# A mixture-of-experts layer on one core: expert weights in loads of 2 MB with 16 KB per partition, eleven slot pairs, and norm 2 vectors and second expert bias on SyncE's queue

## The chip, the cores and the metric

The kernel runs on one core of a Trainium2 chip. The metric is the device time of one execution in microseconds. The kernel before takes 1097.09 us (median of three runs, 1096.65 to 1097.22). TensorE is PE, VectorE DVE, ScalarE ACT, GpSimd POOL, and SyncE SP; SP does nothing but issue transfers.

## The reference, cut to what matters

One encoder layer on 256 tokens of 1,024 features, all in float32: gated linear attention, a residual layer norm, a mixture of 32 experts of which each token takes four, and a second residual layer norm.

```python
h = _gla_mixer(x, w_in, gate_w2, gate_b, norm_g, w_out)        # 4 heads, key 128, value 256
x = _layer_norm(ALPHA * x + h, ln1_g, ln1_b)
logits = x @ router_w + router_b
top_v, top_i = lax.top_k(logits, 4); gates = softmax(top_v)
for e in range(32):
    y = _clamped_swiglu(x @ w_gu[e] + b_gu[e]) @ w_down[e] + b_down[e]   # w_gu[e] 1024x2048, w_down[e] 1024x1024
    out = out + combine[:, e:e+1] * y
x = _layer_norm(ALPHA * x + out, ln2_g, ln2_b)
```

All 32 experts have tokens, so all weights of `w_gu` (268 MB) and `w_down` (134 MB) pass from HBM to SBUF once: 402.65 MB.

## The kernel before

**Stages.** The attention comes first (to about 130 us), then the first norm, the router and the gather of the tokens of expert 0 (to about 155 us), then a loop over the 32 experts, and the second norm with its stores. In the loop the at most 64 tokens of an expert are gathered by 48 small matmuls with `xp` (the tokens in three bfloat16 parts) as the stationary operand (`gather`, L750), go through `first_product` (L769: 64 matmuls, `pgu`, into two PSUM banks), `swiglu` (L787, with four transposes `paT`), and `second_product` (L803: 32 matmuls, `py`), and are scattered into four banks `acc` that stay open over all experts. The gather of expert e+1 and the scatter of expert e-1 stand between the two products. `last_expert` (L817) has finer steps, and the second norm follows it.

**Weights.** A "chunk" is 1 MiB, 128 partitions of 8 KB. Expert e has 12: eight of `w_gu` (128 rows of 2,048 values, one row of 8 KB to a partition, contiguous) and four of `w_down` (256 rows, two rows of 4 KB to a partition). `weight` (L78) issues one DMA per chunk on SP's queue. In the last expert the four `w_down` chunks hold half rows, in runs of 2 KB, and the last of them comes as two DMAs.

**Slots.** 23 slots of 1 MiB (`slot`, L38, tags s0 to s22) hold everything big: the attention's inputs, weights and results first, and then the weight chunks. `order` (L74) is the order in which the slots are taken for weights. `load_next` (L109) issues the next chunk into the next slot of the ring; the issue waits on SP until the slot's last reader is done. 11 chunks of expert 0 are issued from places inside the attention, and four loads of the output projection `wo` (`load_wo`, L405) stand among them, in slots 21, 2, 15 and 12. The rest of the first 23 is issued at L876. From there each consumed chunk is followed by one `load_next`. SP works strictly in order, and a DMA also waits until the eighth DMA before it on the queue has landed (eight semaphores in turn).

**Other vectors.** Norm 2's scale and shift are read on ACT's queue as two rows, after the load of chunk 324; four matmuls and four copies (L975 to L981, end of expert 29) spread them over 128 partitions; `rows` and `ln2` take two slots of the ring for this. The second expert bias `bdn` is loaded on ACT's queue in expert 0 (L734) and used by eight matmuls in expert 1 (L957).

**Overflow.** After expert 30 a branch (L885) looks whether an expert has more than 64 tokens; with these inputs it is not taken.

The order of the work is the order of the code: nothing is rescheduled.

Of the kernel before, what the change touches and what calls it, by code (L numbers as in the profile page):

```python
# [20 lines left out]
NSLOT = 23  # L21
NCH = 12
# [3 lines left out]
def encoder_kernel(ctx, tc, x, ln1_g, ln1_b, ln2_g, ln2_b, w_in, gate_w2, gate_b, norm_g, w_out,  # L26
# [4 lines left out]
    ring = ctx.enter_context(tc.tile_pool(name="ring", bufs=1))  # L31
# [6 lines left out]
    def slot(i, name, shape=(P, 2048), dt=F32):  # L38
        return ring.tile(list(shape), dt, name=name, tag=f"s{i}")
# [34 lines left out]
    order = [3, 18, 20, 6, 11, 7, 9, 4, 19, 13, 14, 21, 22, 2, 15, 5, 12, 17, 8, 16, 10, 1, 0]  # L74
# [3 lines left out]
    def weight(s, name, e, c, last=False):  # L78
        if last and c >= 8:
            t = slot(s, name, (P, 4, 512))  # L80
            h, j = divmod(c - 8, 2)
            n = 1 + (c == 11)
            for i in range(n):
                m = 4 // n
                sync.dma_start(t[:, i * m:(i + 1) * m, :],
                               dram(w_down, e * D * D + (j * 4 + i * m) * P * D + h * 512,
                                    [[D, P], [P * D, m], [1, 512]]))
            return t
        if c < 8:
            t = slot(s, name, (P, 2 * D))  # L90
            src = dram(w_gu, 0, [[2 * D, P], [1, 2 * D]])
            o = c * P * 2 * D
            big = D * 2 * D
        else:
            t = slot(s, name, (P, 2, D))
            src = dram(w_down, 0, [[D, P], [P * D, 2], [1, D]])
            o = (c - 8) * 2 * P * D
            big = D * D
        src = bass.AP(tensor=src.tensor, offset=src.offset + o + e * big, ap=[list(a) for a in src.ap])
        sync.dma_start(t, src)  # L100
        return t

    def next_slot():
        order.append(order.pop(0))
        return order[-1]

    late = {}

    def load_next():  # L109
        i = nload[0]  # L110
        if i == NCH * (NE - 5) and "ln2" not in late:
            if "rows" in late:
                late["ln2"] = slot(order.pop(0), "ln2", (P, 2, D))
                return
            late["rows"] = rows = slot(order.pop(0), "rows", (2, D))
            act.dma_start(rows[0:1], dram(ln2_g, 0, [[D, 1], [1, D]]))
            act.dma_start(rows[1:2], dram(ln2_b, 0, [[D, 1], [1, D]]))
        elif i < NCH * NE:
            chunks[i] = weight(next_slot(), f"w{i}", i // NCH, i % NCH, i // NCH == NE - 1)
            nload[0] += 1  # L120

# [13 lines left out]
    lnr = mis[:16, 1712:1840]  # L135
# [30 lines left out]
    sync.dma_start(rw, dram(router_w, 0, [[NE, P], [P * NE, 8], [1, NE]]))  # L166
    sync.dma_start(rbb, dram(router_b, 0, [[0, P], [1, NE]]))
    sync.dma_start(lnr[0:8], dram(ln1_g, 0, [[P, 8], [1, P]]))
    sync.dma_start(lnr[8:16], dram(ln1_b, 0, [[P, 8], [1, P]]))
# [43 lines left out]
    n = 0  # L213
# [47 lines left out]
    for c in range(4):  # L261
        hi, lo = wqk[c]
        for h in range(H):
            for j in range(2):
                cs = slice(j * 512 + h * DK, j * 512 + (h + 1) * DK)
                for kk in range(2):
                    k = 2 * c + kk
                    mm3(pqk[h][:, j * L:(j + 1) * L], hi[:, kk, cs], lo[:, kk, cs], xT[0][:, k, :], xT[1][:, k, :],
                        j == 0 and k == 0, k == 7)
        if c == 1:  # L270
            pt = bank(0, "plnT")
            pe.transpose(pt[:, :16], lnr, ident[:16, :16])
            dve.tensor_copy(lnT, pt[:, :16])
# [39 lines left out]

    for _ in range(4):
        load_next()
# [102 lines left out]

    vv = []
    score_level(-1)  # L420
    score_store(-1)
    for lev in range(7):
        score_level(lev)
        advance(lev)
        if lev == 0:
            load_next()
        proj(2 * lev)
        step(dve)
        if lev == 1:
            act.dma_start(bp, bass.AP(tensor=bd.tensor, offset=bd.offset, ap=[[2 * D, 96], [1, 2 * D]]))  # L430
        proj(2 * lev + 1)
        if lev < 6:
            step(dve)
        if lev == 1:
            vv.append(slot(8, "vv", (P, 2, D)))
        elif lev == 4:
            load_wo(21)
        elif lev == 5:
            load_wo(2)
        elif lev < 6:  # L440
            load_next()
            if lev == 2:
                load_next()
    step_wo(5, pool)
    load_wo(15)
# [6 lines left out]
    load_next()  # L452
    load_next()
    preload(AF.Sigmoid)
    proj(14)
    load_wo(12)
# [293 lines left out]
    def gather(pcol, xg):  # L750
# [18 lines left out]
    def first_product(chunk, xg, pgl, bias, after=None, between=None, split=False):  # L769
# [3 lines left out]
        for k in range(8):  # L773
            w = chunk(k)
# [6 lines left out]
            if after:  # L781
                after()
# [4 lines left out]
    def swiglu(pgl, aT, post=()):  # L787
# [6 lines left out]
        for c in range(4):  # L794
            if c % 2 == 0:
                cs = slice(c * P, (c + 2) * P)
                dve.tensor_mul(s[:, cs], l[:, cs], s[:, cs])  # L797
            pe.transpose(pb[:, c * P:(c + 1) * P], s[:, c * P:(c + 1) * P], ident)  # L798
# [4 lines left out]
    def second_product(chunk, y, aT, after=None):  # L803
        py = misc("py")
        for c in range(4):
            w = chunk(8 + c)
            for j in range(2):
                kk = 2 * c + j
                a0 = (kk % 4) * P + (kk // 4) * CAP
                for h in range(2):  # L810
                    mm(py[h * 64:(h + 1) * 64, :], aT[:, a0:a0 + CAP], w[:, j, h * 512:(h + 1) * 512],
                       kk == 0, kk == 7)
            if after:
                after()
        act.activation(y, py, AF.Copy)  # L815

    def last_expert(pgl, chunk, after):  # L817
# [16 lines left out]
        def quarter(h, c, i):  # L834
            w = chunk(8 + 2 * h + c)
# [40 lines left out]
    while nload[0] < NSLOT:  # L876
        load_next()

# [3 lines left out]
    def overflow():  # L882
        hold = order[:4]
        many = nc.values_load(cnt[0:1, 0:1], min_val=0, max_val=L)
        with tc.If(many > CAP):  # L885
# [4 lines left out]
            with tc.For_i(0, NE, 1) as e:  # L890
                pg = work.tile([P, 2, 2], F32, name="pg", bufs=1)
                row = slot(hold[2], "row", (1, 2 * D))
# [8 lines left out]
                for r in range(1, L // CAP):  # L901
                    dve.tensor_scalar(pg[:, 0, :], pg[:, 0, :], float(CAP), None, op0=OP.subtract)
                    p_, g_ = (lambda t: pg[:, 0, t:t + 1]), (lambda t: pg[:, 1, t:t + 1])
                    own = slot(hold[3], "own")
# [5 lines left out]
                    def chunk(c):  # L910
                        return weight(hold[c % 2], f"o{r}_{c}", e, c)
# [12 lines left out]
    for e in range(NE):  # L924
# [23 lines left out]
        if e == 0:  # L948
            open_tiles()
            pt = misc("pgT")  # L950
# [24 lines left out]
        if e == NE - 3:  # L975
            rows, ln2 = late["rows"], late["ln2"]
            for j in range(2):
# [10 lines left out]
    z = slot(next_slot(), "z", (P, 2, D))  # L988
# [64 lines left out]
```

## Time and profile before

| | us |
|---|---|
| median of three runs | 1097.09 |
| the profiled execution, own time | 1101.22 |
| its span | 1099.4 |
| PE / DVE / ACT busy in the span | 1007.1 / 292.4 / 156.8 |
| DMA queue 1 (all of SP's and most transfers), share of 16 engines | 94.9% |
| w_gu loads, issue to landing (median of 256) | 19.9 |
| PE waiting for a w_gu load, in total | 61.5 |

A share of DMA is the time that packets took, over 16 engines; it can pass 1 because packets overlap a little. A packet is one contiguous run of one partition's data. "idle before <-X" names what ended an engine's idle time. Times of single executions differ by some microseconds from the median, as the profiled one does here.

### The profile page before, as it was taken

What the parts mean: (1) busy time and instruction counts of PE and PEld (TensorE: products, weight loads), DVE (VectorE), ACT (ScalarE), POOL (GpSimd) and SP (SyncE); (2) the same over time, 40 slices, a digit from 0 to 9 for tenths busy, and PEclk for the clock granted to TensorE, in tenths of its full rate; (3) what the DMA queues carried; (4) which work ended last, traced back from release to release, by engine and by line L of the source; (5) the groups of instructions that cost most, each with busy time, mean ns of one, the idle gap of its engine ahead of it and who ended that gap; (6) DMA issues with size and microseconds to landing.
All of it is one profiled execution on the core that took longest, in us unless ns stands there. A gap on an engine that the chain in (4) does not pass through costs nothing. (4 is left out here: it accounts for less than half of the span.)

```text
span 1099.4 us, 14219 instructions
## 1 busy us (share of the span) xinstructions
PE 1007.1 (92%) x6002; PEld 432.5 (39%) x6002; DVE 292.4 (27%) x639; ACT 156.8 (14%) x272; POOL 43.2 (4%) x45
## 2 busy tenths in 40 slices
PE   7999979999999999989899988888899998888995
PEld 6988743433333333323333333322233333333331
DVE  4786574112111122101111111110111111111104
ACT  5545431000000000000000000000000000000102
POOL 4202320000000000000000000000000000000001
PEclk8999989999999999999999999999999999999998
DMA  9956689999999999999999999999999999999992
GB/s 340 351 200 215 265 317 368 418 417 417 416 416 417 417 415 417 416 418 418 417 417 417 417 416 416 417 417 417 417 418 418 417 417 417 416 416 417 416 398 99
DMA packets 82954, 425.24 MB, mean 387 GB/s; under 512 B 8979, under 2 KB 9763, under 8 KB 50118
## 3 DMA queue, kind: packets, MB, share of 16 engines
q1 hardware_dynamic: 81936, 422.23, 94.9%
q10 hardware_dynamic: 950, 2.04, 0.6%
q8 instruction: 49, 0.80, 0.3%
q14 instruction: 19, 0.16, 0.0%
HBM read 422.81 MB, written 1.44 MB: 386 GB/s over the span
## 5 line engine op out<-in xcount | busy, mean ns | idle before, releaser
L51 PE MATMUL pgu<-w,sx 128*64 128x512 f32 (+1 forms) x2056 | 476.1, 601 | 62.0 <-DMA w<-in_moe_w_gu_dram 61.5
L51 PEld LDWEIGHTS pgu<-w,sx 128*64 128x64 f32 x2056 | 140.9, 137 | 378.2 <-issue 227.4
L51 PE MATMUL py<-w,ya 128*64 128x512 f32 x1024 | 227.2, 595 | 1.4 <-ACT ya L799 0.9
L789 DVE TENSOR_SCALAR gl<-pgu 128x512 f32<-128x512 f32 x31 | 21.4, 691 | 675.2 <-PE pgu L51 675.2
L51 PEld LDWEIGHTS py<-w,ya 128*64 128x64 f32 x1024 | 70.9, 137 | 151.9 <-issue 124.6
L51 PE MATMUL pxg<-oh,xp 128*128 128x64 bf16 x1536 | 51.4, 194 | 1.6 <-DVE oh L616 0.7
L51 PEld LDWEIGHTS <-xp 128*128 128x128 bf16 x1536 | 50.4, 99 | 4.3 <-issue 3.2
L815 ACT ACTIVATE ya<-py 128x512 f32<-128x512 f32 x31 | 18.5, 597 | 231.8 <-PE py L51 231.8
L767 ACT ACTIVATE wgf<-pW 128x256 f32<-128x256 f32 x16 | 6.1, 384 | 270.4 <-PE pW L766 270.4
L767 ACT ACTIVATE wT<-pW 128x256 f32<-128x256 f32 x16 | 6.1, 382 | 253.2 <-PE pW L766 253.2
L51 PE MATMUL pvo<-step,xTh 128*128 128x512 f32 x128 | 40.2, 395 | 0.0
L1016 POOL TENSOR_TENSOR z<-z,ln 128x512 f32<-128x512 f32 x1 | 1.3, 1265 | 938.8 <-ACT z L1014 938.8
L51 PE MATMUL acc<-ya,wT 64*128 64x512 f32 x128 | 36.1, 641 | 0.0
L51 PE MATMUL acc<-ya,wgf 64*128 64x512 f32 (+1 forms) x124 | 36.1, 641 | 0.0
L799 ACT ACTIVATE ya<-paT 128x512 f32<-128x512 f32 x31 | 18.5, 597 | 67.3 <-PE paT L798 67.3
L748 DVE TENSOR_TENSOR sx<-sx,lnT 128x256 f32<-128x256 f32 x64 | 27.2, 425 | 2.2
L747 DVE TENSOR_TENSOR sx<-pxg,lnT 128x256 f32<-128x256 f32 x64 | 26.7, 418 | 0.2 <-PE pxg L51 0.2
L797 DVE TENSOR_TENSOR sx<-gl,sx 128x256 f32<-128x256 f32 x62 | 23.7, 422 | 6.7 <-ACT sx L790 3.6
L51 PEld LDWEIGHTS pvo<-step,xTh 128*128 128x128 f32 x128 | 23.5, 188 | 4.4
L51 PE MATMUL pvo<-step,xTl 128*128 128x512 f32 x64 | 24.9, 389 | 0.0
L51 PE MATMUL ph<-wos,o2T 128*128 128x512 f32 x96 | 23.9, 398 | 0.7 <-ACT o2T L59 0.7
L791 DVE TENSOR_SCALAR gl<-pgu 128x512 f32<-128x512 f32 x31 | 21.4, 691 | 5.0 <-PE pgu L51 5.0
(235 smaller groups left out, 691.0 us busy)
## 6 DMA issues: line engine op xcount, KB each, us to landing
w<-in_moe_w_gu_dram SPq DMA_DIRECT2D x256, 1024.0 KB, 19.9
w<-in_moe_w_down_dram SPq DMA_DIRECT2D x127, 1024.0 KB, 20.0
wqk<-in_gla_w_in_dram SPq DMA_DIRECT2D x4, 1024.0 KB, 10.8
wv<-in_gla_w_in_dram SPq DMA_DIRECT2D x4, 1024.0 KB, 7.1
wog<-in_gla_w_in_dram SPq DMA_DIRECT2D x4, 1024.0 KB, 7.4
wo<-in_gla_w_out_dram SPq DMA_DIRECT2D x4, 1024.0 KB, 7.7
xs<-in_x_dram SPq DMA_DIRECT2D x4, 256.0 KB, 5.1
w<-in_moe_w_down_dram SPq DMA_DIRECT2D x2, 512.0 KB, 14.0
```

Source lines behind the costliest of these rows:

```text
L51: pe.matmul(o, l, r, start=start, stop=stop, skip_group_check=True)
L747: dve.tensor_mul(o, i, g)
L748: dve.tensor_add(o, o, b)
L767: return lambda: act.activation(wT, pb[:, :L], AF.Copy)
L789: dve.tensor_scalar(g, pgl[0], 7.0, None, op0=OP.min)
L791: dve.tensor_scalar(l, pgl[1], 7.0, -7.0, op0=OP.min, op1=OP.max)
L797: dve.tensor_mul(s[:, cs], l[:, cs], s[:, cs])
L799: act.activation(aT, pb, AF.Copy)
L815: act.activation(y, py, AF.Copy)
L1016: pool.tensor_mul(zh, zh, ln2[:, 0, halves[1]])
```

## The change

Expert weights now come in pairs of chunks: 2 MiB, 16 KB per partition, each partition's 16 KB contiguous in HBM. For `w_gu` partition p of pair c holds rows 256c+2p and 256c+2p+1; for `w_down` it holds four consecutive rows. An expert has six such loads (`NCH` 6), and there are eleven pair slots and one single slot. The contraction index of a matmul therefore steps through every second row (fourth row for `w_down`), so the other operand is read with that step: `column_block` picks every second column of `xs` and of `xp` for the transposes and the gathers, and `swiglu` transposes every fourth column of its result, after one DVE product over 512 columns instead of two over 256. The router weights and the first norm's vectors are laid out the same way. In the last expert the last `w_gu` pair comes as two DMAs of 8 KB runs, and each `w_down` pair as two or three DMAs of 2 KB runs, as before.

The 23 slots are declared in a pool of their own in the order (11, 7), (4, 9), (19, 21), (2, 15), (12, 13), (14, 22), (3, 18), (20, 6), (5, 17), (16, 8), (1, 10), 0. It is closed after the gather of expert 0, and the ring's eleven pairs r0 to r10 and the single slot lie at those addresses. All first loads of weights are issued there; none stands inside the attention any more. The four `wo` loads are issued before the attention's levels, into slots 3, 18, 20 and 6. Norm 2's vectors are loaded once behind the first eleven pairs, on SP's queue, spread over 128 partitions by the DMA (2 x 0.5 MB) into the single slot; the four matmuls and copies are gone. `bdn` is loaded on SP's queue.

```diff
-NSLOT = 23
-NCH = 12
+NPAIR = 11
+NCH = 6
...
+    for i in (11, 7, 4, 9, 19, 21, 2, 15, 12, 13, 14, 22, 3, 18, 20, 6, 5, 17, 16, 8, 1, 10, 0):
+        slot(i, f"home{i}")
...
+    def weight(t, e, c, last=False):
+        if last and c >= 4:
+            for i in range(2):
+                n = 1 + (c == 5 and i == 1)
+                for q in range(n):
+                    m = 4 // n
+                    sync.dma_start(t[:, i, q * m:(q + 1) * m, :],
+                                   dram(w_down, e * D * D + (i * 4 + q * m) * P * D + (c - 4) * 512,
+                                        [[D, P], [P * D, m], [1, 512]]))
             return t
+        src, o, big = (w_gu, c * 2 * P * 2 * D, D * 2 * D) if c < 4 else (w_down, (c - 4) * 4 * P * D, D * D)
+        if last and c == 3:
+            for i in range(2):
+                sync.dma_start(t[:, i, :], dram(src, o + e * big + i * 2 * D, [[4 * D, P], [1, 2 * D]]))
         else:
+            src = bass.AP(tensor=src.tensor, offset=src.offset + o + e * big, ap=[[4 * D, P], [1, 4 * D]])
+            sync.dma_start(t.rearrange("p j n -> p (j n)"), src)
...
+    def column_block(a, k):
+        return a.rearrange("p (c q j) -> p c j q", c=4, j=2)[:, k // 2, k % 2, :]
...
-    for _ in range(4):
-        load_next()
...
+    for i in (3, 18, 20, 6):
+        load_wo(i)
...
-                mm(pb[:, k * CAP:(k + 1) * CAP], xp[:, i // 3, i % 3, k * P:(k + 1) * P], oh[:, i // 3, :],
+                mm(pb[:, k * CAP:(k + 1) * CAP], column_block(xp[:, i // 3, i % 3, :], k), oh[:, i // 3, :],
                    i == 0, i == 5)
...
         for k in range(8):
-            w = chunk(k)
+            w = chunk(k // 2)[:, k % 2, :]
...
-            if after:
+            if after and k % 2:
                 after()
...
+        dve.tensor_mul(s, l, s)
+        for r in range(4):
+            pe.transpose(pb[:, r * P:(r + 1) * P], s.rearrange("p (q r) -> p r q", r=4)[:, r, :], ident)
...
-    while nload[0] < NSLOT:
+    early.close()
+    ring.append(ctx.enter_context(tc.tile_pool(name="ring", bufs=1, side="right", reuse_waits="tile")))
+    while nload[0] < NPAIR:
         load_next()
+    ln2 = ring[0].tile([P, 2, D], F32, name="ln2", tag="single")
+    for j, a in enumerate((ln2_g, ln2_b)):
+        sync.dma_start(ln2[:, j, :], dram(a, 0, [[0, P], [1, D]]))
...
             open_tiles()
+            sync.dma_start(tmp["bdn"], dram(b_down, 0, [[D, NE], [1, D]]))
...
-        if e == NE - 3:
-            rows, ln2 = late["rows"], late["ln2"]
-            for j in range(2):
-                for c in range(2):
-                    pb = misc("pln2")
-                    mm(pb, ident[0:2, j:j + 1].to_broadcast([2, P]), rows[:, c * 512:(c + 1) * 512], True, True)
-                    act.activation(ln2[:, j, c * 512:(c + 1) * 512], pb, AF.Copy)
```

**On SP's queue during the attention**, before: behind the last attention weights come nine expert chunks, with the `wo` loads among what follows. The names in brackets are what each issue waits for: DMAHW is an earlier landing, the others are readers of the slot.

```order
L100 DMA w_525<-in_moe_w_gu_dram 128x2048 [waits DMAHW3_49,PE_49,Pool_49]
L100 DMA w_527<-in_moe_w_gu_dram 128x2048 [waits DMAHW6_49]
L100 DMA w_529<-in_moe_w_gu_dram 128x2048 [waits DMAHW7_49,PE_49]
L100 DMA w_531<-in_moe_w_gu_dram 128x2048 [waits DMAHW2_49,DMAHW0_49,DVE_49]
L100 DMA w_567<-in_moe_w_gu_dram 128x2048 [waits DMAHW1_49,DVE_49]
L100 DMA w_603<-in_moe_w_gu_dram 128x2048 [waits DMAHW3_49,DVE_49]
L100 DMA w_705<-in_moe_w_gu_dram 128x2048 [waits DMAHW5_49,DMAHW4_49,DVE_49]
L100 DMA w_707<-in_moe_w_gu_dram 128x2048 [waits DMAHW5_49,PE_49]
L100 DMA w_762<-in_moe_w_down_dram 128x2x1024 [waits DMAHW6_49,DVE_49]
L408 DMA wo_817<-in_gla_w_out_dram 128x4x512 [waits DMAHW7_49,DVE_49]
```

The same place after the change:

```order
L414 DMA wo_552<-in_gla_w_out_dram 128x4x512 [waits DMAHW2_49,PE_49,Pool_49]
L414 DMA wo_554<-in_gla_w_out_dram 128x4x512 [waits DMAHW6_49]
L414 DMA wo_556<-in_gla_w_out_dram 128x4x512 [waits DMAHW7_49,PE_49]
L414 DMA wo_558<-in_gla_w_out_dram 128x4x512 [waits DMAHW0_49,DVE_49]
L110 DMA w_1359<-in_moe_w_gu_dram 128x4096 [waits DMAHW4_49,DMAHW3_49,DVE_49]
L110 DMA w_1361<-in_moe_w_gu_dram 128x4096 [waits DMAHW5_49,DVE_49]
L110 DMA w_1363<-in_moe_w_gu_dram 128x4096 [waits DMAHW6_49,DVE_49]
L110 DMA w_1365<-in_moe_w_gu_dram 128x4096 [waits DVE_49,DMAHW7_49,PE_49,Pool_49]
L110 DMA w_1367<-in_moe_w_down_dram 128x4096 [waits DMAHW0_49,DMAHW1_49,DVE_49,PE_49]
L110 DMA w_1369<-in_moe_w_down_dram 128x4096 [waits DMAHW1_49,PE_49]
```

The four `wo` loads take the place of the first four chunks, and every weight load is twice as large and waits for the readers of two slots.

**On SP's queue at the start of the expert loop**, after the change, the vectors of norm 2 stand behind the eleventh pair (w_1379) and `bdn` (L944) behind the fifteenth (w_1460). Before, neither was on this queue.

```order
L110 DMA w_1379<-in_moe_w_down_dram 128x4096 [waits DMAHW6_49,PE_49]
L871 DMA ln_1381<-in_ln_g_dram 128x1024 [waits DVE_49,DMAHW7_49,PE_49,Pool_49]
L871 DMA ln_1381<-in_ln_b_dram 128x1024 [waits DMAHW0_49]
L110 DMA w_1401<-in_moe_w_down_dram 128x4096 [waits DMAHW1_49,PE_49]
L110 DMA w_1421<-in_moe_w_gu_dram 128x4096 [waits DMAHW2_49,PE_49]
L110 DMA w_1448<-in_moe_w_gu_dram 128x4096 [waits DMAHW3_49,PE_49]
L110 DMA w_1460<-in_moe_w_gu_dram 128x4096 [waits DMAHW4_49,PE_49]
L944 DMA bdn<-in_moe_b_down_dram 32x1024 [waits DMAHW5_49,DVE_49]
```

Both are queued in order with the weights, so a wait of theirs holds the next pair back.

**On PE at the end of expert 29**, before: the second product takes four chunks, and the spread of the norm's rows (`pln`) stands ahead of expert 30's bias.

```order
L798 MATMUL paT<-ident,sx 128x128 x4
L51 MATMUL acc<-ya,wT 128x512 x2
L51 MATMUL py<-w_5900,ya 64x512 x4
L51 MATMUL py<-w_5913,ya 64x512 x4
L51 MATMUL py<-w_5919,ya 64x512 x4
L51 MATMUL py<-w_5925,ya 64x512 x4
L51 MATMUL pln_6223<-rows,ident 128x512
L51 MATMUL pln_6226<-rows,ident 128x512
L51 MATMUL pln_6229<-rows,ident 128x512
L51 MATMUL pln_6232<-rows,ident 128x512
L51 LDWEIGHTS sel
```

After the change:

```order
L788 MATMUL paT<-ident,sx 128x128 x4
L59 MATMUL acc<-ya,wT 128x512 x2
L59 MATMUL py<-w_5543,ya 64x512 x8
L59 MATMUL py<-w_5560,ya 64x512 x8
L59 LDWEIGHTS sel
```

The matmuls of the two products are as many as before, each load feeds twice as many, and `pln` is gone.

## Rows read from the trace of the kernel before

**Rows 1.** Stretches: PE, PEld, DVE, ACT, POOL busy (instructions), granted clock, DMA share, GB/s
```profile
0.00:60.00 60.00, 53.29 (x331) 48.38 (x332) 37.16 (x68) 31.01 (x42) 19.09 (x30) 0.94 0.93 344
60.00:153.00 93.00, 86.96 (x485) 73.38 (x483) 65.05 (x113) 47.37 (x81) 21.28 (x13) 0.98 0.66 247
153.00:190.00 37.00, 34.75 (x203) 13.47 (x202) 21.70 (x46) 6.42 (x13) 0.00 (x0) 0.91 0.85 321
190.00:1060.00 870.00, 804.98 (x4876) 288.21 (x4874) 155.90 (x390) 65.42 (x124) 0.00 (x0) 1.00 1.02 417
```

**Rows 2.** Who PE waited for, 400 to 1080 us: us in total, times, longest us
```profile
PE pgu L51 <- DMA w<-in_moe_w_gu_dram: 61.5, 111, 1.7
```

**Rows 3.** PE in order of time, expert 2: start us, us, operation, count
```profile
216.11 0.60 PE L51 MATMUL pgu<-bp,sel 96*64 96x512 bf16 x4
216.54 13.90 PE L51 MATMUL pgu<-w,sx 128*64 128x512 f32 x64
...
230.65 1.56 PE L51 MATMUL pxg<-oh,xp 128*128 128x64 bf16 x48
...
234.85 7.09 PE L51 MATMUL py<-w,ya 128*64 128x512 f32 x32
241.77 0.60 PE L51 MATMUL pgu<-bp,sel 96*64 96x512 bf16 x4
```

**Rows 4.** Stretches in which only 8 KB runs, or only 4 KB runs, flow
```profile
230.00:246.00 16.00, 16.00 (x120) 6.60 (x118) 3.99 (x9) 2.10 (x4) 0.00 (x0) 1.00 1.01 420
250.00:256.50 6.50, 6.24 (x32) 1.89 (x28) 0.19 (x1) 0.00 (x0) 0.00 (x0) 1.00 1.02 409
...
381.00:397.00 16.00, 16.00 (x117) 6.36 (x114) 5.20 (x13) 1.50 (x3) 0.00 (x0) 1.00 1.01 420
401.60:407.00 5.40, 5.40 (x28) 1.85 (x26) 0.00 (x0) 0.00 (x0) 0.00 (x0) 1.00 1.03 410
```

**Rows 5.** DMA packets of 230 to 246 us, and of 250 to 256.5 us
```profile
DMA packets 921, 6.72 MB, mean 420 GB/s; under 512 B 102, under 2 KB 102, under 8 KB 102
DMA packets 686, 2.66 MB, mean 409 GB/s; under 512 B 37, under 2 KB 37, under 8 KB 686
```

**Rows 6.** The page's DMA: all packets; the queue of instruction fetches (packets, MB, share)
```profile
DMA packets 82954, 425.24 MB, mean 387 GB/s; under 512 B 8979, under 2 KB 9763, under 8 KB 50118
...
q8 instruction: 49, 0.80, 0.3%
```

**Rows 7.** SP's queue: when loads were issued (start us, us to the last issue's end, count)
```profile
86.25 8.91 SPq L408 DMA_DIRECT2D wo<-in_gla_w_out_dram  x3
...
119.72 0.34 SPq L100 DMA_DIRECT2D w<-in_moe_w_gu_dram  x1
...
143.57 0.90 SPq L100 DMA_DIRECT2D w<-in_moe_w_down_dram  x2
153.24 6.45 SPq L100 DMA_DIRECT2D w<-in_moe_w_down_dram  x2
161.11 21.09 SPq L100 DMA_DIRECT2D w<-in_moe_w_gu_dram  x8
183.59 5.95 SPq L100 DMA_DIRECT2D w<-in_moe_w_down_dram  x4
```

**Rows 8.** POOL's last piece of wo, in order of time
```profile
130.61 2.39 POOL L60 TENSOR_TENSOR wos<-wo,wos 128x1024 fp32r<-128x1024 f32 x1 [2.99 <-ACT wos L59]
```

**Rows 9.** PE in order of time, expert 29 to the end of the last first product
```profile
1022.29 3.78 PE L51 MATMUL pln<-rows,ident 2*128 2x512 f32 x8
...
1056.27 0.62 PE L51 MATMUL pgu<-bp,sel 96*64 96x512 bf16 x4 [2.73 <-PEq L885]
...
1068.68 5.38 PE L51 MATMUL pgu<-w,sx 128*64 128x512 f32 x32
```

**Rows 10.** Attention scores, level 0 (every second column read) and whole columns: min/median/max ns
```profile
L51 PE MATMUL psc<-QT,KQ x16: 334/337/337, 48.3 to 50.8; 128*128 128x128 f32 x16
...
L51 PE MATMUL psc<-KQ x16: 273/275/275, 46.5 to 48.2; 128*128 128x128 f32 x16
```

More of the change, by code (lines that the diff above doesn't have):

```diff
@@ L1 @@
+from contextlib import ExitStack
 import concourse.bass as bass
@@ L29, in encoder_kernel @@
     dve, act, pe, pool, sync = nc.vector, nc.scalar, nc.tensor, nc.gpsimd, nc.sync
-    ring = ctx.enter_context(tc.tile_pool(name="ring", bufs=1))
+    early = ExitStack()
+    slots = early.enter_context(tc.tile_pool(name="slots", bufs=1, side="right"))
     fixed = ctx.enter_context(tc.tile_pool(name="fixed", bufs=1))
@@ L38, in slot @@
     def slot(i, name, shape=(P, 2048), dt=F32):
-        return ring.tile(list(shape), dt, name=name, tag=f"s{i}")
+        return slots.tile(list(shape), dt, name=name, tag=f"s{i}")
+    for i in (11, 7, 4, 9, 19, 21, 2, 15, 12, 13, 14, 22, 3, 18, 20, 6, 5, 17, 16, 8, 1, 10, 0):
+        slot(i, f"home{i}")
     def keep(shape, name, dt=F32, tag=None):
@@ L71, in copy @@
             dve.tensor_copy(o, a)
-    order = [3, 18, 20, 6, 11, 7, 9, 4, 19, 13, 14, 21, 22, 2, 15, 5, 12, 17, 8, 16, 10, 1, 0]
+    ring = []
+    order = list(range(NPAIR))
     chunks = {}
     nload = [0]
[L78 to L87, printed above, removed]
-            return t
[L89 to L93, printed above, removed]
-        else:
[L95 to L100, printed above, removed]
-        return t
@@ L103, in next_slot, with pair, hold_pair @@
[L103 to L107, printed above, removed]
+    def pair(name, shape):
+        order.append(order.pop(0))
+        return hold_pair(order[-1], name, shape)
+    def hold_pair(j, name, shape):
+        return ring[0].tile([P, *shape], F32, name=name, tag=f"r{j}")
+    def weight(t, e, c, last=False):
[7 more added lines that the diff above has]
+                                        [[D, P], [P * D, m], [1, 512]]))
+            return t
+        src, o, big = (w_gu, c * 2 * P * 2 * D, D * 2 * D) if c < 4 else (w_down, (c - 4) * 4 * P * D, D * D)
+        if last and c == 3:
+            for i in range(2):
+                sync.dma_start(t[:, i, :], dram(src, o + e * big + i * 2 * D, [[4 * D, P], [1, 2 * D]]))
+        else:
+            src = bass.AP(tensor=src.tensor, offset=src.offset + o + e * big, ap=[[4 * D, P], [1, 4 * D]])
+            sync.dma_start(t.rearrange("p j n -> p (j n)"), src)
+        return t
@@ L109, in load_next, with chunk_shape @@
+    def chunk_shape(c, last=False):
+        return (2, 2 * D) if c < 4 else (2, 4, 512) if last else (4, D)
     def load_next():
         i = nload[0]
[L111 to L119, printed above, removed]
+        if i < NCH * NE:
+            e, c = divmod(i, NCH)
+            last = e == NE - 1
+            chunks[i] = weight(pair(f"w{i}", chunk_shape(c, last)), e, c, last)
@@ L424, in encoder_kernel @@
         advance(lev)
-        if lev == 0:
-            load_next()
         proj(2 * lev)
@@ L804, in second_product @@
         py = misc("py")
-        for c in range(4):
-            w = chunk(8 + c)
-            for j in range(2):
-                kk = 2 * c + j
-                a0 = (kk % 4) * P + (kk // 4) * CAP
+        for c in range(2):
+            w = chunk(4 + c)
+            for r in range(4):
+                a0 = r * P + c * CAP
                 for h in range(2):
-                    mm(py[h * 64:(h + 1) * 64, :], aT[:, a0:a0 + CAP], w[:, j, h * 512:(h + 1) * 512],
-                       kk == 0, kk == 7)
+                    mm(py[h * 64:(h + 1) * 64, :], aT[:, a0:a0 + CAP], w[:, r, h * 512:(h + 1) * 512],
+                       c + r == 0, c + r == 4)
             if after:
@@ L882, in overflow @@
     def overflow():
-        hold = order[:4]
+        hold = order[:3]
         many = nc.values_load(cnt[0:1, 0:1], min_val=0, max_val=L)
@@ L891, in overflow @@
                 pg = work.tile([P, 2, 2], F32, name="pg", bufs=1)
-                row = slot(hold[2], "row", (1, 2 * D))
+                own = hold_pair(hold[2], "own", (4 * D,))
+                row = own[0:1, 2 * D:]
                 with nc.allow_non_contiguous_dma(reason="a column"):
@@ L987, in encoder_kernel @@
     nb2 = work.tile([P, 1], F32, name="nb2", bufs=1)
-    z = slot(next_slot(), "z", (P, 2, D))
+    z = pair("z", (2, D))
     halves = [slice(0, 512), slice(512, 1024)]
```

44 lines of the change are left out of this document (13 added, 31 removed).

## The prediction, made before the changed kernel ran

> **What bounds the kernel now.** I read the stretches first. From 190 to 1060 us the 16 DMA engines are full (share 1.02) at a steady 417 GB/s, while before that they are not: 0.93, 0.66 and 0.85 of three stretches [rows 1]. PE looks busy too, at 805 of 870 us, so the second view is whom PE waits for: in 111 pieces, 61.5 us in all, for `w_gu` loads [rows 2]. The third view is PE's own time for an expert whose weights are already there. In expert 2 it is 25.7 us from one bias matmul (216.11) to the next (241.77), without a wait [rows 3]. An expert is 12.58 MB, which takes the DMA 30.2 us at 417 GB/s. So PE is faster than the queue by some 4.5 us an expert, eats up the lead of the filled ring, and then waits. The loop is bound by the transfers, and the time is: when the queue becomes full for good, plus the bytes that are left over the rate, plus what follows the last `w_gu` chunk.
>
> The end has to be checked by itself. PE spends 3.8 us on the spread of the norm's rows at 1022, 2.7 us in the branch, and finishes the first product of expert 31 at 1074.1 [rows 9]. How far behind the last landing that is, no row says. With 4.5 us of slack an expert against 3.8 and 2.7 us lost, I take it that PE and the queue about meet there, so what the queue gains the end gains.
>
> **Part 1, longer runs.** The trace has pure stretches: between 230 and 246 us hardly a packet is under 8 KB, between 250 and 256.5 us all are [rows 5]. Six 8 KB stretches lie at 419 to 421 GB/s and six of 4 KB at 407 to 411; two of each are shown [rows 4]. With means of 420.2 and 409.3 a packet holds one of 16 engines for 8192 x 16 / 420.2 = 311.9 ns, or 4096 x 16 / 409.3 = 160.1 ns. Two of 4 KB cost 8.3 ns more than one of 8 KB, so that is what a packet costs beyond its bytes. A 16 KB packet is then 2 x 311.9 - 8.3 = 615.5 ns. Before, an expert is 64 packets of 8 KB and 64 of 4 KB per engine, 30.21 us; after, it is 48 of 16 KB, 29.54 us. That is 0.67 us less for each expert, and a pair takes 8 x 615.5 ns = 4.92 us.
>
> How many experts are left when the queue is full for good? By 190 us the stretches moved 344 x 60 + 247 x 93 + 321 x 37 = 55.5 MB. Of the 425.2 MB in all [rows 6], 402.65 are expert weights and 1.05 the stores, so some 21 MB of the 55.5 were other things: 34.5 MB, or 33 of the 1 MiB chunks. 347 remain to the last `w_gu` chunk (the 380th), 28.9 experts: 28.9 x 0.67 = 19.4 us gained. The last expert's `w_down` keeps its 2 KB runs.
>
> No row shows a 16 KB packet on this queue. The nearest below is that the step from 8 to 16 KB gives nothing (623.8 ns): then only `w_down` gains, 30.21 - 48 x 623.8 ns = 0.27 us an expert, 7.8 us. The nearest above is that the rate climbs again by as much as from 4 to 8 KB, to 431 GB/s: 608 ns, 29.19 us, 1.02 an expert, 29.5 us. The only 16 KB packets that the page has are the instruction fetches: 49 of them in 0.3% of 16 x 1099.4 us [rows 6], 1.08 us each. [...] I take 615.5.
>
> [...]
>
> **Part 2, the start.** Before, chunks go out singly as slots come free; after, a pair needs both. SP takes the pairs in order, so what counts is the release of the late ones. I assume the attention keeps its pace and read the releases off SP's issues before [rows 7]. `wo` moves from 86 us (when its first old slot came free) to the place of the first chunks; in exchange slots 21, 2, 15 and 12 are free for weights at once. The pair (3, 18) is free when DVE is done with the second `wo` piece, 119.7; (20, 6) when POOL ends the last, 130.61 + 2.39 = 133.0 [rows 8]; (5, 17), (16, 8) and (1, 10) by 143.6. From 133.0 the queue holds four pairs, 19.7 us, to 152.7. Slot 0 comes free at 153.2, and the 1 MB of norm 2's vectors runs from there for about 2.7 us: it falls into a gap, since the next pair waits for expert 0's second chunk, at 161.1. The next pairs follow about every 5.2 us (eight chunk issues from 161.1 to 182.2), each 4.92 us long, and the one after at 183.6. So 15 pairs, 30 chunks, are in by 183.6, when the queue is nearly dry, and about 32 by 190, against 33 before. From there PE frees a pair in 3.5 us (a quarter of 13.90), the queue stays full, and the start costs one chunk, 2.5 us. Covers: the vectors of norm 2 cost 2.5 us more if slot 0 were free only after 158; `bdn` is needed by expert 1's end of the first product near 201 and queues behind at most one or two pairs at 176, so it lands in time.
>
> **Part 3, PE.** Every second column of `xp`, `xs` and every fourth of the swiglu result is read with a step. The trace has one such read: scores of level 0 read every second fp32 column, 337 ns a matmul against 275 for whole columns [rows 10]. With 62 ns for each of the 48 gather loads, and three times as much for each of four transposes, an expert costs PE up to 3.0 + 0.75 = 3.7 us more; nothing is the other end (bfloat16 at a step of two covers the bytes of whole fp32). Beside 29.54 - 25.7 = 3.8 us of slack this costs nothing in the loop in either case. On the way into expert 0 it isn't covered: 48 such loads and a few transposes, 0 to 3 us. I take 1, nearer to nothing. DVE's one product for two is beside PE's scatter. The gone `pln` matmuls save 3.8 us of PE at expert 29, where PE again has slack.
>
> [...]
>
> **Part 4, the end.** A pair of `w_gu` lands as one, so PE's first product of expert 30 ends 3.5 us behind its last landing instead of 1.75; the branch follows with no wait to absorb it. The last pair of expert 31 is split in two. I add 1.75 us. Everything behind is as before, 25 us.
>
> **Sum**, on the profiled execution: 1101.2 - 19.4 + 2.5 + 1 + 1.75 = 1087.1, that is 14.1 us less. The profiled run stands 4.1 us above the median; the same 14.1 off 1097.1 gives **1083 us**.
>
> **Rivals.**
> 1. *No gain beyond 8 KB.* For it: one doubling only is measured. Against: the packet cost shows in all twelve stretches. 14.1 - (19.4 - 7.8) = 2.5 us gained: 1094.6. 14%. [...]
> 2. *The rate climbs on.* For it: 409 to 420 is a step of 11. Against: a fixed cost per packet must give half as much with each doubling. 10 us more: 1073. 10%.
> 3. *PE becomes the bound.* The steps in the gather loads and the transposes make an expert longer than the queue's 29.5 us. With a price of 3.7 us PE is at 29.4; if the four-column step or the loads cost somewhat more, say 4.2 in all, it is at 29.9: from the start of expert 2 [rows 3] that is 216 + 1 + 29 x 29.9 + 16 = 1100 for the end of the last first product, with its branch, against 1074, a loss of 26: 1123. It turns slower than before at about 3.3 us (216 + 1 + 29 x 29.0 + 16 = 1074). For it: rows 10 and a PE with at most 4 us to give. Against: at one price per 128 columns even the upper end barely gets there, and bfloat16 halves the bytes. 10%.
> 4. *The pool's change holds all loads back.* If the new ring waited for the whole old pool, the first pair would go out at 153.2, and 190 pairs x 4.92 + 153.2 + 2 = 1090 for the last `w_gu`, against some 190 + 28.9 x 30.2 = 1063 now: 27 us more, 1124. Against: the first pair's waits name DVE and landings alone, neither PE nor POOL, which read the late slots. 4%.
>
> **How the numbers follow.** My forecast has 62%, with 1077 to 1090 as its own range: the start 0 to 5 us, the steps 0 to 3, the packet cost 0.6 to 0.8 us an expert. With rival 1 and part of rival 2 the range is 1072 to 1097; above it lies most of rivals 3 and 4. A difference of 0.2%, 2.2 us, is what a measurement of this kernel tells from none. Faster: all of the forecast, all of rival 2, and two thirds of rival 1, 81%. Same: the rest of rival 1 and a crossing of rival 3, 5%. Slower: 14%.
>
> **What would show it.** The full stretch should show 425 to 426 GB/s for 417, with all weight packets at 16 KB, and PE still waiting for `w_gu` from about expert 11 on. The mean share from 60 to 153 us may fall, but by 190 us the bytes moved should be within 2 MB of 55.5. The gather should take between 1.6 and 4.6 us. A rate of 420 or less says rival 1; no waits of PE for loads says rival 3; a queue without weights before 150 us says rival 4.

## The result, and the profile after

The changed kernel takes **1084.57 us** (median of 4 runs, 1083.93 to 1086.53) against 1097.15 for the kernel before on the same chip: a ratio of 0.9884 with a 95% interval of 0.9865 to 0.9903. On a second chip, against 1098.47, it was 1084.77 us, 0.9877 (0.986 to 0.9893). The forecast was 1083 with a range of 1072 to 1097.

The stretches of the kernel after, in the columns of [rows 1] (busy time of PE, PEld, DVE, ACT and POOL, granted clock, DMA share, GB/s):

```profile
0.00:60.00 60.00, 53.76 (x338) 48.24 (x339) 39.34 (x71) 31.91 (x44) 20.18 (x30) 0.97 0.92 338
60.00:153.00 93.00, 87.25 (x497) 73.90 (x496) 64.62 (x113) 48.00 (x81) 21.38 (x13) 0.96 0.66 250
153.00:190.00 37.00, 35.52 (x197) 12.61 (x196) 20.16 (x42) 4.83 (x12) 0.00 (x0) 0.96 0.89 342
190.00:1040.00 850.00, 785.03 (x4850) 295.30 (x4848) 153.66 (x360) 63.04 (x120) 0.00 (x0) 1.00 1.01 426
```

Whom PE waited for, and the page's DMA line, which answer to [rows 2] and [rows 6]:

```profile
PE pgu L59 <- DMA w<-in_moe_w_gu_dram: 61.5, 58, 1.7
```

```profile
DMA packets 39618, 426.23 MB, mean 394 GB/s; under 512 B 5465, under 2 KB 6241, under 8 KB 15106
```

The full queue moves 426 GB/s for 417, with less than half the packets. PE still waits 61.5 us for `w_gu`, in 58 pieces for 111, as a pair lands as one load: the transfers are the bound, as before.

Expert 2, against [rows 3], and the end, against [rows 9] (PE in order of time: start, us, operation, count, wait before it):

```profile
213.66 0.60 PE L59 MATMUL pgu<-bp,sel 96*64 96x512 bf16 x4
214.10 13.90 PE L59 MATMUL pgu<-w,sx 128*64 128x512 f32 x64
...
228.21 1.56 PE L59 MATMUL pxg<-oh,xp 128*128 128x64 bf16 x48
...
230.76 0.75 PE L788 MATMUL paT<-ident,sx 128*128 128x128 f32 x4
...
239.42 0.60 PE L59 MATMUL pgu<-bp,sel 96*64 96x512 bf16 x4
...
1016.86 3.65 PE L59 MATMUL pgu<-w,sx 128*64 128x512 f32 x16 [1.34 <-DMA w<-in_moe_w_gu_dram]
1021.67 3.65 PE L59 MATMUL pgu<-w,sx 128*64 128x512 f32 x16 [1.16 <-DMA w<-in_moe_w_gu_dram]
...
1039.23 0.62 PE L59 MATMUL pgu<-bp,sel 96*64 96x512 bf16 x4 [2.32 <-PEq L879]
...
1051.64 5.38 PE L59 MATMUL pgu<-w,sx 128*64 128x512 f32 x32
```

An expert without a wait is 25.76 us (213.66 to 239.42) for 25.66; the steps have cost it 0.1 us. The gather is 1.56 us as before. The first product of the last expert ends at 1057.0 for 1074.1, 17.0 us earlier. That is more than the medians show (12.6), because the two profiled executions did not start alike: 1101.22 was high among the runs of before, and the run e7 below gives a better partner.

### The profile page after: what moved, and what is told of

It reads as the page before. It is cut to its first block, busy times and chain, and to the rows that moved or that the text cites. A ratio compares the mean times of both kernels' runs of the same rounds, so it can differ in the third digit from the quotient of the medians.

```text
span 1082.2 us, 13732 instructions
## 1 busy us (share of the span) xinstructions
PE 991.6 (92%) x5995; PEld 440.2 (41%) x5995; DVE 290.4 (27%) x608; ACT 154.4 (14%) x268; POOL 44.4 (4%) x45
## 5 line engine op out<-in xcount | busy, mean ns | idle before, releaser
L59 PE MATMUL pgu<-w,sx 128*64 128x512 f32 (+1 forms) x2056 | 461.9, 596 | 62.2 <-DMA w<-in_moe_w_gu_dram 61.5
L59 PEld LDWEIGHTS pgu<-w,sx 128*64 128x64 f32 x2056 | 146.4, 137 | 358.7 <-issue 281.0
L781 DVE TENSOR_SCALAR gl<-pgu 128x512 f32<-128x512 f32 x31 | 21.4, 691 | 663.1 <-PE pgu L59 663.1
L788 PEld LDWEIGHTS paT<-ident,sx 128*128 128x128 f32 x124 | 17.3, 209 | 23.1 <-DVE sx L739 22.0
L788 PE MATMUL paT<-ident,sx 128*128 128x128 f32 x124 | 23.2, 310 | 0.2 <-DVE sx L786 0.2
## 6 DMA issues: line engine op xcount, KB each, us to landing
w<-in_moe_w_down_dram SPq DMA_DIRECT2D x3, 1024.0 KB, 31.1
```

The costliest lines, as they stand in the source:

```text
L59: pe.matmul(o, l, r, start=start, stop=stop, skip_group_check=True)
L781: dve.tensor_scalar(g, pgl[0], 7.0, None, op0=OP.min)
L788: pe.transpose(pb[:, r * P:(r + 1) * P], s.rearrange("p (q r) -> p r q", r=4)[:, r, :], ident)
```

## The experiments

**e1: the pairs in halves.** Everything of the change but the run length: each pair is two loads of 8 KB runs.

```diff
-            sync.dma_start(t.rearrange("p j n -> p (j n)"), src)
+            flat = t.rearrange("p j n -> p (j n)")
+            for i in range(2):
+                sync.dma_start(flat[:, i * 2 * D:(i + 1) * 2 * D],
+                               dram(src, o + e * big + i * 2 * D, [[4 * D, P], [1, 2 * D]]))
```

> The changed kernel with one thing undone: each pair keeps its place and its rows, but comes as two loads of 1 MB whose runs are 8 KB. If the packet length is what the change gained by, an expert is 96 packets of 311.9 ns, 29.94 us for 29.52, the full stretch moves 420 GB/s for 426, and the time is 28.9 x 0.42 = 12 us longer: about 1096.5 us. If the gain came from the pairs, the new start or the moved vectors, it stays at 1084.6 and 426 GB/s.

Measured: 1103.41 us (1100.98 to 1104.4), 1.005 (1.0033 to 1.0067) against before. The gain is gone, and more than the run length went with it: the size was missed by some 7 us. Its stretches:

```profile
60.00:153.00 93.00, 86.44 (x493) 72.52 (x494) 64.59 (x114) 47.33 (x80) 21.39 (x13) 0.96 0.52 203
...
190.00:1040.00 850.00, 788.63 (x4762) 284.20 (x4759) 150.32 (x352) 61.22 (x117) 0.00 (x0) 1.00 1.01 419
```

and whom SP's queue waited for:

```profile
SPq L111 <- DMA ln1g<-in_ln_g_dram: 30.1, 1, 30.1
```

The full queue is at 419 GB/s for 425 to 426, which over 28.9 experts is 12 us against e0 and 14 to 15 against the first profile: this is the run length's part, near what was expected. The rest was lost in the attention: 203 GB/s for 250 from 60 to 153 us, and 1.2 to 1.5 MB less by 190 us, some 3 us. For 30.1 us an SP load was held until the load of norm 1's vector `ln1g`, which ACT issues, had landed. Run e8 takes up that wait.

**e2: the old runs.** Pairs, vectors and ring of the change, but 8 KB and 4 KB runs, the old order of the contraction and no stepped reads:

```diff
-            src = bass.AP(tensor=src.tensor, offset=src.offset + o + e * big, ap=[[4 * D, P], [1, 4 * D]])
-            sync.dma_start(t.rearrange("p j n -> p (j n)"), src)
+            src = bass.AP(tensor=src.tensor, offset=src.offset + o + e * big, ap=[[row, P], [P * row, n], [1, row]])
+            sync.dma_start(t, src)
```

> The changed kernel with loads of 2 MB in eleven pairs, but each load made of the old runs: 8 KB of w_gu and 4 KB of w_down, with the old order of the contraction rows and no stepped reads on PE. Packet length as the cause: 417 GB/s and 30.2 us an expert, 28.9 x 0.67 = 19 us longer, about 1104 us, that is slower than the kernel before by its later start. Rival, larger and fewer loads as the cause: 426 GB/s and 1084.6 us. Rival, stepped reads cost something that the packets hid: the loss is smaller than 19 us.

Measured: 1105.39 us (1104.6 to 1106.97), 1.0063 (1.0046 to 1.0079).

```profile
190.00:1040.00 850.00, 767.45 (x4728) 285.12 (x4726) 148.93 (x350) 60.91 (x116) 0.00 (x0) 1.00 1.02 416
```

As expected: the full queue is back at the old rate, the other parts of the change make the kernel slower (6.9 us over before on this chip), and all of the gain comes from the runs.

**e3: the transfers alone.** No computation (the output is zeros): five stretches of the same weight loads on SP's queue, with runs of 2, 4, 8, 16 and 32 KB.

> Transfers alone, no computation (the output is zeros): five stretches of 50 MB, in runs of 2, 4, 8, 16 and 32 KB per packet, all in loads of 2 MB but the last, which has 4 MB. A fixed 8.3 ns a packet on top of the bytes gives 389, 409, 420, 426 and 429 GB/s. The rival that the rate climbs by equal steps gives 431 and 442 for the last two. If a packet has a limit at 16 KB, the last stretch equals the one before it.

Measured, in the same order (DVE and POOL busy, clock, DMA share, GB/s):

```profile
20.00:110.00 90.00, 0.00 (x0) 0.00 (x0) 1.00 1.05 387
140.00:220.00 80.00, 0.00 (x0) 0.00 (x0) 1.00 1.03 410
260.00:340.00 80.00, 0.00 (x0) 0.00 (x0) 1.00 1.01 422
380.00:460.00 80.00, 0.00 (x0) 0.00 (x0) 1.00 1.01 429
500.00:590.00 90.00, 0.00 (x0) 0.00 (x0) 1.00 1.00 431
```

From 4 to 8 KB it is 12 GB/s, to 16 KB 7 more, to 32 KB 2 more. As time of a packet on one of 16 engines (bytes x 16 / rate) these are 84.7, 159.8, 310.6, 611 and 1216 ns: two packets cost 9 to 11 ns more than one of twice their size up to 16 KB, and some 6 at the last step, where 0.5 GB/s of rounding is worth up to 3 ns. The gain shrinks with each doubling, as a fixed cost per packet makes it.

**e5: the pool without waits by tile.** The new ring then waits for the whole old pool:

```diff
-    ring.append(ctx.enter_context(tc.tile_pool(name="ring", bufs=1, side="right", reuse_waits="tile")))
+    ring.append(ctx.enter_context(tc.tile_pool(name="ring", bufs=1, side="right")))
```

> The changed kernel, but the new ring waits for the whole old pool, so that the first pair goes out when the last old slot is free, near 151 us instead of 55. If the loop is bound by the queue, all of the lead is lost: 151.5 + 2 + 2.7 + 190 x 4.92 = 1091 us for the last w_gu pair on the mean engine, against 1044, so about 1084.6 + 47 = 1131 us. If the early loads only fill a ring that PE does not need so soon, the loss is that of expert 0 waiting for its first pair, 6 to 10 us: about 1093.

Measured, one run: 1128.74 us.

```profile
60.00:153.00 93.00, 87.01 (x493) 73.64 (x492) 64.83 (x113) 47.82 (x81) 21.40 (x13) 0.96 0.06 19
...
190.00:1040.00 850.00, 758.62 (x4616) 284.80 (x4614) 143.87 (x338) 59.46 (x113) 0.00 (x0) 0.98 1.01 426
```

The full stretch keeps its 426 GB/s, and what is lost is the lead of the loads during the attention: 44 us. By 190 us SP's queue had moved 34.09 MB for 54.44 in e0, and the 20.35 MB are 47.8 us at 426 GB/s.

**e0: the changed kernel again**, beside e4 and e6 on their chip.

> The changed kernel as it is, on the chip of the two runs beside it, as the kernel to hold them against: 0.9885 of the kernel before, about 1085 to 1086 us.

Measured: 1084.77 us (1084.62 to 1085.59).

**e4: norm 2's vectors late.** Their two loads behind expert 19:

```diff
-    for j, a in enumerate((ln2_g, ln2_b)):
-        sync.dma_start(ln2[:, j, :], dram(a, 0, [[0, P], [1, D]]))
...
+        if e == 19:
+            for j, a in enumerate((ln2_g, ln2_b)):
+                sync.dma_start(ln2[:, j, :], dram(a, 0, [[0, P], [1, D]]))
```

> The changed kernel with norm 2's two loads (1 MB) issued behind expert 19 instead of ahead of expert 0. If they lay in a gap of the queue before, they now cost their own time in the full stretch, 1.05 MB at 426 GB/s: 2.5 us more than the changed kernel. If they were in the way of the weights at the start already, it makes no difference.

Measured: 1086.12 us (1083.51 to 1087.68), 0.9884 (0.9864 to 0.9904), 1.35 us over e0 with intervals that overlap: the direction fits, but the times don't decide it. What SP's queue had moved by 190 us, in e4 and then in e0 (packets, MB, share of the stretch):

```profile
q1 hardware_dynamic: 10363, 52.91, 74.4%
```

```profile
q1 hardware_dynamic: 10681, 54.44, 75.2%
```

Without the 1.05 MB of vectors no more weights came in early. That alone does not decide it, since the clock of the first 60 us was 0.94 in e4 and 1.00 in e0, and PE began expert 0's first product at 154.94 in e4 and at 151.82 in e0. A row of e0 does (in the columns of [rows 1]; norm 2's two loads were issued at 149.45 and 149.83):

```profile
156.00:158.00 2.00, 2.00 (x10) 0.65 (x8) 1.93 (x3) 0.00 (x0) 0.00 (x0) 0.88 0.00 0
```

The vectors are in, the queue is empty, and the next pair goes out at 157.80, after a wait for PE: at the start they lie in a gap.

**e6: the pair of expert 30 in two**, as that of expert 31 is already:

```diff
-        if last and c == 3:
+        if c == 3 and (last or (isinstance(e, int) and e == NE - 2)):
```

> The changed kernel with the last w_gu pair of expert 30 as two loads of 1 MB (8 KB runs), as the last expert's already is. If PE is late at the end because it gets that pair as one, it starts on the first half 2.4 us earlier and everything behind comes 1.5 to 1.8 us earlier, since from there PE waits for no load. If the end hangs on the landing of the last w_gu pair, nothing changes (0.1 us at most, for the shorter runs).

Measured: **1082.85 us** (1081.54 to 1084.01), 0.9855 (0.9839 to 0.9872), 1.9 us under e0. PE at the end of expert 30 and into 31:

```profile
1011.77 3.65 PE L59 MATMUL pgu<-w,sx 128*64 128x512 f32 x16 [0.52 <-DMA w<-in_moe_w_gu_dram]
1016.76 7.09 PE L59 MATMUL pgu<-w,sx 128*64 128x512 f32 x32 [1.34 <-DMA w<-in_moe_w_gu_dram]
...
1038.29 0.62 PE L59 MATMUL pgu<-bp,sel 96*64 96x512 bf16 x4 [2.85 <-PEq L879]
```

The 1.16 us wait at 1021.67 is gone, which bears out the end's term. From its start on the third pair to the end of the first product PE takes 7.09 us for 8.46 in e0. The intervals of e6 and e0 overlap a little, and 0.6 us of the difference is there before that (1016.76 for 1017.38), so the size is known to a us only. This version is the fastest measured, ahead of both kernels.

**e7: the kernel before, profiled again**, unchanged.

> The kernel before, profiled once more, because its first profiled execution stood 4 us above its median. Draw: the 417 GB/s (350.16 MB in 840 us, 416.9) and the clock of the start differ between executions; a new profile has a time of 1097 to 1099 us, and the 2 to 4 us less are seen either in the stretch from 190 to 1030 us (418 to 418.5 GB/s) or by 190 us (0.5 to 1 MB more on SP's queue than 53.26 MB). Rival: the first profile was typical of a profiled execution, 416.9 GB/s and 53.3 MB again, and 1101 us.

Measured: 1098.7 us; on this chip 17 runs of before lie between 1095.74 and 1101.55. The first and the last stretch of [rows 1] again, and SP's queue by 190 us (53.26 MB in the first profile):

```profile
0.00:60.00 60.00, 53.48 (x348) 48.39 (x349) 42.56 (x74) 32.89 (x44) 20.03 (x30) 1.00 0.95 358
...
190.00:1040.00 850.00, 789.50 (x4748) 282.07 (x4746) 151.06 (x379) 63.32 (x120) 0.00 (x0) 0.99 1.02 416
```

```profile
q1 hardware_dynamic: 14820, 54.77, 76.4%
```

The draw was mainly at the start: with the clock at 1.00 for 0.94 PE began expert 0's first product at 151.72 for 155.60, and 1.5 MB more were in by 190 us, 3.6 us. The rate did not help: from 190 to 1030 us e7 moved 349.31 MB for 350.16, which gave 2 us back.

**e8 and e9: norm 1's vectors later.** In e1 (as e8) and e6 (as e9) the two loads of ACT's queue stand behind the first ring loads:

```diff
-    act.dma_start(ln1[0], dram(ln1_g, 0, [[0, P], [1, D]]))
-    act.dma_start(ln1[1], dram(ln1_b, 0, [[0, P], [1, D]]))
...
     while nload[0] < NPAIR:
         load_next()
+    act.dma_start(ln1[0], dram(ln1_g, 0, [[0, P], [1, D]]))
+    act.dma_start(ln1[1], dram(ln1_b, 0, [[0, P], [1, D]]))
```

> The kernel of two loads a pair, with the two loads of norm 1's vectors from ACT's queue moved behind the first ring loads in program order. Theory (a load of SP was held 30 us because it takes its turn on the same landing semaphore as ln1g): the wait of SP for ln1g goes, the stretch from 60 to 153 us comes back from 203 to about 250 GB/s, SP's queue has moved 54.3 MB by 190 us for 52.96, and the time is 3 us less than 1103.4, about 1100.4. Rival (twice as many loads fill the eight landings and are late whatever the vectors do): 203 GB/s and 1103 stay. Still above before in either case if the queue at 419 GB/s is what it costs: not under 1098.

> The changed kernel with the last w_gu pair of expert 30 split, and the loads of norm 1's vectors moved as in the run before. Theory: the 15.5 us for which the sixth pair waited for ln1g cost nothing, since the pairs behind it were not free sooner and the queue ran dry at 144 us anyway: 1083, within 1.5 us of the version with the split alone, and SP's queue at 54.2 MB by 190 us. Rival: the 15.5 us were a loss of the lead: up to 1 MB more by 190 us, 2.5 us, 1080.5.

Measured: e8 1131.97 us (1127.75 to 1133.5), 1.029 (1.0264 to 1.0316); e9 1100.15 us (1095.99 to 1101.36), 1.0008 (0.9995 to 1.0021). Both expectations were wrong in direction: the wait did not go, it grew. e9's wait of SP's queue, and the load of `ln1g` with the SP load that follows it:

```profile
SPq L110 <- DMA ln1g<-in_ln_g_dram: 36.4, 1, 36.4
```

```profile
L867 ACTq DMA_DIRECT2D ln1g<-in_ln_g_dram x1: 345/345/345, 152.3 to 152.3; - x1
...
DMA to landing us min/median/max: 3.8/3.8/3.8
```

```profile
156.12 0.33 SPq L110 DMA_DIRECT2D w<-in_moe_w_gu_dram  x1
```

`ln1g` is issued at 152.3, lands 3.8 us later, and the held load goes out at 156.12. In the changed kernel itself it is issued at 118.0, takes 4.0, and the held pair goes out at 122.03. So the hold ended with that landing in both places, which is what the theory says: loads of both queues take their turn on the same landing semaphores. In the changed kernel's profile the loads of SP's queue name semaphores 100 to 107 and ACT's 101 to 106; `ln1g` and the held pair both name 102, while the eighth load before that pair on its own queue (a `wo`, issued at 45.00) names 107. In the loop of the kernel before it is the eighth load: the one issued at 440.07 names 107, as does the one of 419.94, which landed at 440.01. A load on SP's queue thus waited not only for the eighth load before it on its own queue. What failed was the remedy. ACT comes to the moved loads only at 152 us, and the SP load that had its turn behind them, the eighth pair in e9, went out at 156.12, where the changed kernel's goes out at 131.66.

The two also give the price of the lead a second time. e9 had 46.67 MB on SP's queue by 190 us for 54.23 in e6: 7.56 MB at 426 GB/s are 17.7 us, and its median is 17.3 above e6's. For e8 the same sum gives 33.5 us (38.91 MB for 52.96, at 419) against 28.6 by the medians. The bytes are those of the profiled executions, and between these it is 31.1 (spans 1130.3 and 1099.2); the 2.4 us that are left stay open.

## Why the prediction was right

The best like-with-like pair is e7 and e0, one profiled execution each, on two chips: both had the granted clock at 1.00 for the first 60 us, and PE began expert 0's first product at 151.72 and 151.82. Their spans are 1096.9 and 1083.0 us, 13.9 apart, against a sum of 14.1.

**Part 1, longer runs: right.** From 190 to 1030 us e7 moved 349.31 MB and e0 357.18: 415.8 and 425.2 GB/s, so an expert of 12.58 MB takes 30.26 and 29.59 us. That is 0.67 us each, as predicted, and 28.9 of them make 19.4. e3 shows the same price per packet without any computation, and e1 and e2 show that nothing else brings the gain.

The fixed cost measured is 8 to 11 ns a packet (8.3 in the prediction, 9 to 11 in e3 up to 16 KB); what it consists of no run here shows. The 1.08 us of an instruction fetch [rows 6] say nothing of these packets: 16 KB of weights took 0.61 us in e3.

**Part 2, the start: right, near its size.** e0's 54.44 MB on SP's queue by 190 us hold 1.18 MB (norm 2's vectors and `bdn`) that were not on it before. That leaves 53.26 against 54.77 in e7: 1.5 MB behind, or 3.6 us at 425 GB/s, where 2.5 was predicted. The gap for norm 2's vectors was there (e4). The working took all waits of the ring's loads to be slot releases and missed a held pair: the seventh (not the sixth, as e9's expectation has it), in slots 3 and 18, waited 15.5 us for `ln1g`. That wait made none of the 1.5 MB, as the changed kernel's trace shows (DVE's and POOL's pieces of `wo`, the queue, and the issue of the eighth pair):

```profile
117.11 1.23 DVE L68 TENSOR_TENSOR wos<-wo,wos 128x1024 fp32r<-128x1024 f32 x1
129.24 2.39 POOL L68 TENSOR_TENSOR wos<-wo,wos 128x1024 fp32r<-128x1024 f32 x1 [2.99 <-ACT wos L67]
130.00:132.00 2.00, 2.00 (x15) 1.78 (x13) 1.08 (x2) 0.54 (x1) 1.63 (x1) 1.00 0.00 0
131.66 0.33 SPq L110 DMA_DIRECT2D w<-in_moe_w_gu_dram  x1
```

Slot 18 came free at 118.3, when DVE was done with it, so the hold to 122.03 cost 3.7 us of the 15.5. The pair was in by 130, the queue stood empty, and the eighth pair waited for POOL until 131.6. So the pair's delay cost nothing, and the missing 1.5 MB lie elsewhere: the working had a chunk of it for the waits for two slots at once, and the other 0.5 MB stay open.

**Part 3, PE: the value near nothing was right.** By form, the weight loads of the gather, of the swiglu result's transposes and of the attention's last transposes, after (mean ns of one after the count and busy time):

```profile
L59 PEld LDWEIGHTS <-xp 128*128 128x128 bf16 x1536 | 50.4, 99 | 4.7 <-issue 3.7 <-ACT xp L581 0.7
...
L788 PEld LDWEIGHTS paT<-ident,sx 128*128 128x128 f32 x124 | 17.3, 209 | 23.1 <-DVE sx L739 22.0 <-DVE sx L786 1.0
...
L541 PEld LDWEIGHTS pzT<-ident,xs 128*128 128x128 f32 x16 | 2.5, 207 | 1.0 <-ACT zT L542 0.7
```

Before, these were 99, 141 and 146 ns. So the bfloat16 loads at a step of two cost nothing (99 ns in both), and the fp32 loads cost 60 to 70 ns more, at a step of two (146 to 207) and of four (141 to 209) alike; four such transposes, 0.75 us for 0.66, make the 0.1 us seen in expert 2. The way into expert 0 cost 0.1 us (151.72 to 151.82) for the 1 us taken. Rival 3 had the loads of `xp` at [rows 10]'s fp32 price, and that was its error. That row was also misread: the scores' operand (`qview`) does not step by two. At level 0 it takes one column from each of two places in turn, 1,025 values apart, at level 1 two columns from each, at level 2 four. Levels 1 and 2:

```profile
L51 PE MATMUL psc<-QT,KQ x16: 282/282/286, 56.4 to 58.2; 128*128 128x128 f32 x16
...
L51 PE MATMUL psc<-QT,KQ x16: 270/275/275, 63.8 to 65.5; 128*128 128x128 f32 x16
```

With one column at a time it is 337 ns, with two 282, with four 275, as for whole columns.

**Part 4, the end: right in its term, wrong in what it left out.** For the pair that lands as one 1.75 us were predicted; it is 1.9 by the medians of e0 and e6 and 1.2 by the wait that went. The branch stays on the path in both (2.5 us in e7, 2.6 in e0), and so does all behind it. But the working put the gone `pln` matmuls at nothing, because PE had slack at expert 29, and in the kernel before that slack was used up. PE in e7 from its last wait for a load on, and the clock behind `pln`:

```profile
1006.65 1.94 PE L51 MATMUL pgu<-w,sx 128*64 128x512 f32 x8 [0.58 <-DMA w<-in_moe_w_gu_dram]
...
1020.01 4.39 PE L51 MATMUL pln<-rows,ident 2*128 2x512 f32 x8
1024.33 1.06 PE L51 MATMUL pgu<-bp,sel 96*64 96x512 bf16 x4
1025.18 16.24 PE L51 MATMUL pgu<-w,sx 128*64 128x512 f32 x64
...
1055.89 7.06 PE L51 MATMUL pgu<-w,sx 128*64 128x512 f32 x32
```

```profile
1025.00:1030.00 5.00, 5.00 (x14) 1.38 (x12) 0.00 (x0) 0.03 (x1) 0.00 (x0) 0.51 1.01 419
```

and in e0:

```profile
1022.19 3.65 PE L59 MATMUL pgu<-w,sx 128*64 128x512 f32 x16 [1.16 <-DMA w<-in_moe_w_gu_dram]
...
1040.48 8.76 PE L59 MATMUL pgu<-w,sx 128*64 128x512 f32 x32
```

Before, PE waits for no load after expert 29's. Behind `pln` the granted clock was low (0.51 in that stretch; 0.66 from 1025 to 1030 us in the first profile), and expert 30's first product took 16.24 us for 13.90. By the queue alone, an expert (30.26 us) after 1006.65 and with the 1.94 us of the last chunk, that product would have ended at about 1038.9, an estimate; it ended at 1041.4. So `pln` and the low clock cost 2.6 us on the path, which the change gained (1.0 us by the same estimate in the first profile of before). Whether `pln` brought the clock down no run tests. Against that, PE's work behind the branch took 8.76 us in e0 for 7.06 in e7, a loss of 1.7 that is not of the change: the first profile of before has 8.76 there too, with the granted clock at 0.53 from 1056.8 to 1060 us, and the first of the changed kernel as well, at 0.52 from 1039.8 to 1043.

**Sum.** With the prediction's four terms as measured on e7 and e0 it is 19.4 - 3.6 - 0.1 - 1.8 = 13.9 us, the difference of the spans. That it fits so closely is partly luck. Two small errors in the prediction, the start a us too cheap and PE a us too dear, cancel. Two terms that it does not have, 2.6 gained and 1.7 lost at the end, nearly cancel as well; and the last load that PE waits for in e0 is expert 30's, so that 27.9 experts and 18.7 us count. With these the sum is 18.7 - 3.6 - 0.1 - 1.8 + 2.6 - 1.7 = 14.1.

**The rivals.** The rate did not stay at 420 (rival 1) and did not climb to 431 (rival 2; that rate was seen only at 32 KB, in e3). PE kept its waits (rival 3). The new ring did not wait for the old pool (rival 4: the first pair went out at 55.39 us); when it was made to, in e5, it cost 44 us where the rival had 41 over the forecast.

The first comparison's 17.2 us between profiled spans would have misled a reader into looking for 3 us of a further gain. e7 shows where they come from: 2.5 us lie between the two profiles of the kernel before and 0.8 between those of the changed one.

## What to carry to other kernels

When a loop is bound by a full DMA queue, take the price of a packet from two run lengths that the trace already shows, and halve the gain with each further doubling (23, 12, 7 and 2 GB/s in e3). Count how many bytes are in before the queue is full for good: each MB of that lead is worth its time at the full rate at the end (17.3 us for 7.6 MB in e9). At the end of the kernel, find the last load that the bottleneck's reader waits for in either version: what stands behind it counts in full, as `pln` did (2.6 us with the low clock behind it, by the estimate above). Before believing a difference of a few us between two profiles, compare the granted clock of their first stretch, or profile the old kernel a second time.

## What was not expected of the hardware and the program's queues

A load on SP's queue waited for a load that ACT issued and that shares nothing with it but the turn on a landing semaphore (102 for both in the changed kernel): 15.5 us in the changed kernel, 30.1 in e1, 36.4 in e9 and 61.7 in e8. In the changed kernel this cost nothing, since the slot was free only 3.7 us before the wait ended and the queue ran empty behind it; moving that load later cost 17 and 29 us. A stepped fp32 weight load cost 60 to 70 ns more whether the step was two or four (146 to 207 and 141 to 209), and a bfloat16 one at a step of two nothing (99 and 99). Behind `pln` and behind the branch the granted clock was low for some us (0.51 from 1025 to 1030 us in e7, 0.52 from 1039.8 to 1043 us in the first profile of the changed kernel); PE's work there took 2.3 us longer in e7 (16.24 for 13.90) and 1.7 in the changed kernel (8.76 for 7.06).
